# Two transformer blocks on one NeuronCore: in the mixers, the low part of a weight tile from a second, adding transfer in place of a subtraction

## The chip, the cores and the metric

The kernel runs on one core of a Trainium2 chip, as one program. The metric is the time of one execution on the device in microseconds; the lower the better. The median of three runs counts.

## What is computed

The reference runs two blocks one after the other on 512 tokens of width 1024, all in float32.

```python
def first_block(x, ...):                       # two layers
    for l in range(2):
        x = layer_norm(ALPHA * x + 0.5 * swiglu_ffn(x, ffn1_w_gu[l], ffn1_w_down[l]), ...)
        x = layer_norm(ALPHA * x + hybrid_mixer(x, w_in[l], w_out[l], ...), ...)
        x = layer_norm(ALPHA * x + 0.5 * swiglu_ffn(x, ffn2_w_gu[l], ffn2_w_down[l]), ...)
    return x

def second_block(x, meta_tokens, ...):         # one layer; 16 meta tokens go ahead of the 512
    h = concatenate([meta, x])
    h = h + 0.5 * swiglu(rmsnorm(h), w_gate, w_up, w_down)
    u = rmsnorm(h) @ w_in                      # differential attention and latent top-k attention
    ...
    h = h + concatenate([o_a, o_b]) @ w_out
    h = h + 0.5 * swiglu(rmsnorm(h), w_gate2, w_up2, w_down2)
    return h[16:]
```

`hybrid_mixer` projects with `w_in`, runs sliding-window attention (with sinks) and multi-scale retention side by side, and projects with `w_out`. So there are nine stages: FFN, mixer, FFN twice in the first block, and FFN, mixer, FFN in the second.

## The kernel before

**Precision.** TensorE multiplies in the type fp32r. Every operand is held as a high part (its copy in fp32r) and a low part (the value less that copy), and each product is three matmuls: high by high, high by low, low by high (`mm3`).

**Weights.** All weights lie in DRAM as one stream of 489 raw tiles of 128x1024 float32, 512 KB each, in the order of use. The class `Weights` (lines 56 to 276) brings them in. SyncE loads a raw tile into one of four buffers `wraw` (`_dma`). `_begin` then plans the two steps that make a split tile: ScalarE copies the raw tile to fp32r (high part), and then VectorE or GpSimd subtracts the high part from the raw tile (low part), whichever would be done sooner by the plan's clocks (`advance`). A raw buffer is free for the next load when its last step has been issued (`frees`). A split tile goes into one of four slots `wsplit` of its own, or into a slot `lent` by buffers that the stage does not need at the moment. A slot is free again when the last matmul that reads it is done. Most tiles of the FFNs have other kinds (S0 to S3, `SA`: sums of tiles for a product with seven multiplications in place of eight); in the mixers all tiles have the plain kind "W".

**Order.** The Python program writes each engine's instructions in their final order, and a planner (`Plan`) keeps a clock for each engine with a cost for each operation. `t["P"]` is TensorE's clock, `V`, `S`, `G` those of VectorE, ScalarE and GpSimd, `D` that of the transfers, `L` that of the port VectorE and GpSimd are taken to share. Side work (softmax, normalisation, splits) runs as generators that get their turn when the clocks say they are due (`run_due`, `tick`, `until`). Where the plan sees TensorE idle, `idle` writes filler matmuls (`m<-minus`, `s<-minus`, 128x256, results unused) in number for 0.8 of the gap at 0.118 us each. So any change of a cost or of a step moves the instructions around it, on all engines.

**Names.** `mixer1` (line 1396, called twice) and `mixer2` (line 1811) are the mixers, `ffn` (line 1029) the FFN. `acc`, `s`, `m` are PSUM tiles, `Z` the residual stream, `x` its normalised split, `y` (in the second block `yA`, `yB`) the mixer's output before the last projection, `rsq` a reciprocal root by a power on GpSimd, `pt` probabilities, `tb` a table of biases, `turned` and `sums` tiles of the FFN's special product. Nearly all instructions carry line 429, that of the helper that records them (`Engine`); they are told apart by their tiles.

Of the kernel before, what the change touches and what calls it, by code (L numbers as in the profile page):

```python
# [13 lines left out]
AF = mybir.ActivationFunctionType  # L14
OP = mybir.AluOpType
# [29 lines left out]
NEG = -1.0e30  # L45
GROUPS = ("T", "V", "more", "K1", "ya", "ic")
TAKEN = -3.0e38


class Step:  # L50
    def __init__(self, part, heavy, run, after, ready, frees):
        self.part, self.heavy, self.run, self.after, self.ready, self.frees = part, heavy, run, after, ready, frees
        self.issued, self.end = False, 0.0


class Weights:
# [7 lines left out]
    def __init__(self, nc, pool, kinds, src, plan, scalar, lo_engines):  # L64
        self.nc, self.pool, self.src = nc, pool, src
        self.plan, self.scalar, self.lo_engines = plan, scalar, lo_engines
        self.parts, r = [], 0
        for k in kinds:
            if k == "S0":
                pair, r = (r, r + 1), r + 2  # L70
            if k == "W":
                self.parts.append((k, (r,)))
                r += 1
            else:
                self.parts.append((k, pair))
        self.n_raw = r
        self.raw, self.arrives, self.spent, self.user = {}, {}, set(), {}
        for i, (k, rs) in enumerate(self.parts):
            for x in rs:
                self.user[x] = i  # L80
        self.ready, self.pending, self.chain = {}, [], {}
        self.n_dma = self.n_prep = self.n_get = 0
        self.free = deque(("own", f"w{i}") for i in range(4))
        self.lent, self.used = set(), {}
        self.fence = self.scr = None
        self.scr_last = []

    def lend(self, group, *tiles):

        self.lent.add(group)  # L90
        for t in tiles:
            if isinstance(t, tuple):
                self.free.append((group, t))
            else:
                for i in range(t.shape[1]):
                    self.free.append((group, (t[:, i, 0], t[:, i, 1])))
# [67 lines left out]
    def _begin(self, i, kind, rs, slot):  # L164
        if slot is not None:
            self.free = deque(x for x in self.free if x is not slot)
            self.used[slot[0]] = self.used.get(slot[0], 0) + 1
            if slot[0] == "own":
                t = self.pool.tile([128, 2, 1024], F32R, name="wsplit", tag=slot[1])
                hi, lo = t[:, 0], t[:, 1]  # L170
            else:
                hi, lo = slot[1]
            self.ready[i] = (slot, hi, lo)
        else:
            hi = lo = None
        at = max(self.arrives[r] for r in rs)
        raw = [self.raw.get(r) for r in rs]
        ch = self.chain

        def split(src, n, after=(), frees=(), ready=0.0):  # L180
            h = self._add(i, False, lambda: self.scalar.activation(hi[:, :n], src, AF.Copy), after, ready)
            return self._add(i, True, lambda e: e.tensor_sub(lo[:, :n], src, hi[:, :n]), [h], 0.0, frees)

        if kind == "W":
            split(raw[0], 1024, (), rs, at)
        elif kind == "S0":
            ch["lo"] = split(raw[0], 1024, (), (), at)
        elif kind == "SA":
            a, b = raw
            scr = self.scr  # L190
            one = self._add(i, True, lambda e: e.tensor_sub(scr[:, 512:], a[:, :512], b[:, :512]), self.scr_last, at)
            two = self._add(i, True, lambda e: e.tensor_add(b[:, :512], b[:, :512], b[:, 512:]), [one], at)
            six = self._add(i, True, lambda e: e.tensor_sub(scr[:, :512], b[:, :512], a[:, :512]), [two])
            ch.update(one=one, two=two, six=six)
        elif kind == "S1":
            ch["s1"] = split(self.scr, 1024, [ch["one"], ch["six"]])
        elif kind == "S2":
            split(raw[1], 1024, [ch["two"], ch["six"]], rs[1:])
        else:
            a, scr = raw[0], self.scr  # L200
            four = self._add(i, True, lambda e: e.tensor_sub(a[:, 512:], a[:, 512:], scr[:, :512]), [ch["six"], ch["lo"]])
            split(a[:, 512:], 512, [four], rs[:1])
            self.scr_last = [ch["s1"], four]
# [74 lines left out]
class Plan:  # L278
# [43 lines left out]
    def dma(self, ap, us):  # L322

        start = self.t["D"]
        name = ap.tensor.name
        if name in self.before:
            start = max(start, self._last(self.before.pop(name)) + 1.2)
        self.t["D"] = start + us
        c0 = ap.offset % ap.ap[0][0]
        c1 = c0 + 1 + sum((n - 1) * abs(d) for d, n in ap.ap[1:])  # L330
        self.used.setdefault(name, []).append((0, 128, c0, c1, start + us + 0.9, True, "D"))
        return start + us + 0.9 + self.LAG

    def op(self, e, us, writes, reads, shared=False):

        start = max(self.t[e], self.t["L"]) if shared else self.t[e]
        spans = []
        for ap, w in [(a, True) for a in writes] + [(a, False) for a in reads]:
            name, (ps, pn), free = ap.tensor.name, ap.ap[0], ap.ap[1:]
            if ps == 0:  # L340
                continue
            p0, c0 = divmod(ap.offset, ps)
            c1 = c0 + 1 + sum((n - 1) * abs(d) for d, n in free)
            if name in self.before:
                start = max(start, self._last(self.before.pop(name)) + self.LAG)
            for q0, q1, d0, d1, end, ew, ee in self.used.get(name, ()):
                if (w or ew) and q0 < p0 + pn and p0 < q1 and d0 < c1 and c0 < d1:
                    if ee != e:
                        start = max(start, end + self.LAG)
                    elif e != "P" and ew and not w:  # L350
                        start = max(start, end + 0.12)
            spans.append((name, p0, p0 + pn, c0, c1, w))
        end = self.t[e] = start + us
        if shared:
            self.t["L"] = end
        for name, q0, q1, d0, d1, w in spans:
            u = self.used.setdefault(name, [])
            if w:
                u[:] = [a for a in u if not (q0 <= a[0] and a[1] <= q1 and d0 <= a[2] and a[3] <= d1)]
            u.append((q0, q1, d0, d1, end, w, e))  # L360
        self.cur.end[e] = end
# [95 lines left out]
def build(ctx, tc, t, out, stop=None, dbg=None):  # L457
# [3 lines left out]
    V, S, G, PE = (Engine(plan, k, e) for k, e in zip("VSGP", (nc.vector, nc.scalar, nc.gpsimd, nc.tensor)))  # L461
# [22 lines left out]
    def have(room, shape=(128, 512), dtype=F32):  # L484

        while True:
            until(lambda: room.count() > 0)
            at, now = room.when(1), plan.t["P"]
            if at <= now + 0.2:
                break  # L490
            if not run_due():
                idle(min([at] + [due(j) for j in eligible() if due(j) > now]))
        return room.take(shape, dtype)
# [9 lines left out]
    W = Weights(nc, wpool, t["kinds"], t["w"], plan, S, (V, G))  # L503
# [525 lines left out]
    def ffn(halves, x, norm, newx, turned, source, sink=None, first=((0, 1, 2, 3),)):  # L1029
# [4 lines left out]
        if whole[0][1] > 512:  # L1034
            whole = halves
        n = halves[0][1] - halves[0][0]
        T = turned(n)
        W.take_back(*GROUPS)
        assert W.idle(*GROUPS)
        W.scr = T.scr  # L1040
        W.lend("more", *T.more)
        gates, H = {}, {}
# [63 lines left out]
        def seven(m, i, dst, beside):  # L1106
# [4 lines left out]
            def mult(p, w, k0, b, start):  # L1111
                for k in range(4):
                    mm3(p[:, :n], (w[0][:, k0 + k], w[1][:, k0 + k]), (b[0][:, k], b[1][:, k]),
                        start and k == 0, k == 3, **({} if start else dict(skip_group_check=True)))
                    tick()
# [19 lines left out]
            pb = have(accs)  # L1135
            mult(pb, w1, 0, T.t[2], True)
            j2 = then(over(q[:, 0], s[:, 0], pb, OP.add), j1)
# [9 lines left out]
            pc = have(accs)  # L1147
            mult(pc, w1, 4, T.t[3], True)
            W.done(w1)
            j4 = then(over(q[:, 1], q[:, 0], pc, OP.add), j2)  # L1150
            w2 = W.get("S2", (8, 128))
            pd = have(accs)
            mult(pd, w2, 0, T.t[1], True)
            j5 = then(over(u[:, 1], q[:, 1], pd, OP.add, True), j4)
# [239 lines left out]
        return d  # L1394

    def mixer1(l, x, norm):
        ready = set()
        W.take_back(*GROUPS)
        assert W.idle(*GROUPS)
# [409 lines left out]
    tokq = [(16 + 128 * i, 128) for i in range(4)]  # L1809

    def mixer2(x, norm):
        ready = set()
        W.take_back(*GROUPS)
        assert W.idle(*GROUPS)
# [716 lines left out]
```

## Time and profile before

| | |
|---|---|
| runs | 3102.7, 3108.1, 3113.8 us; median 3108.1 |
| profiled execution | 3105.4 us |
| its span, first to last instruction | 3103.5 us |
| TensorE's mean granted clock | 0.991 of full speed |
| busy share: TensorE, VectorE, ScalarE, GpSimd | 98%, 69%, 44%, 19% |
| mean share of the 16 transfer engines in use; rate | a quarter; 87 GB/s |

The stages lie, in us from the first instruction, at: FFN to 376, mixer to 613, FFN to 990, FFN to 1370, mixer to 1604, FFN to 2000, FFN (second block) to 2397, mixer to 2736, FFN to the end.

The busy time of TensorE includes the fillers, and the ends of its matmuls are modelled: a busy TensorE is not one that does useful work throughout. In a timeline a row gives the start, the time to the end of the group, engine and line, the operation, the written tile and those read, the shape and the count; in square brackets stand the idle time of that engine before it and what ended it.

### The profile page before, as it was taken

To read this page: it belongs to the slowest core of one execution; us is meant where nothing else is said; L and a number is where in the kernel's file an instruction comes from. 1 tells how busy PE (TensorE), PEld (TensorE's weight loads), DVE (VectorE), ACT (ScalarE), POOL (GpSimd) and SP (SyncE) were. 2 spreads that over 40 slices of the span, in tenths; PEclk is the share of its full clock that TensorE was granted. 3 is DMA by queue.
4 is the path that set the end of the run, shared out by engine and by line. 5 is a ranking of instruction groups with operands and counts; after the bars stand their busy time and mean duration, and the time that the engine had idled before them with its cause. 6 is when DMAs were issued, how large, how long until landed. Compare 5 with 4: busy or idle time off the path is not lost.

```text
span 3103.5 us, 51892 instructions
## 1 busy us (share of the span) xinstructions
PE 3043.5 (98%) x20797; PEld 2770.7 (89%) x20797; DVE 2149.0 (69%) x4209; ACT 1366.7 (44%) x2517; POOL 585.6 (19%) x411
## 2 busy tenths in 40 slices
PE   9999999999999999999999999999999999999999
PEld 8999987789999999997779999999999887889997
DVE  6767756587677766874567667486775886477774
ACT  4434464353344433447334434343343445544342
POOL 1121222212212122022321221111102111212110
PEclk9999999999999999999999999999999999999999
DMA  4333221113323233321211333223322110122332
GB/s 147 105 102 102 88 96 62 67 63 103 102 97 108 82 102 102 129 69 62 69 55 50 115 102 105 73 72 103 101 96 91 62 62 28 35 82 96 102 106 86
DMA packets 75553, 269.77 MB, mean 87 GB/s; under 512 B 8445, under 2 KB 10533, under 8 KB 75184
## 3 DMA queue, kind: packets, MB, share of 16 engines
q1 hardware_dynamic: 73712, 261.65, 25.3%
q0 software_dynamic: 1024, 3.75, 0.4%
q8 instruction: 164, 2.69, 0.4%
q10 hardware_dynamic: 576, 1.05, 0.1%
q14 instruction: 77, 0.63, 0.1%
HBM read 264.30 MB, written 3.68 MB: 86 GB/s over the span
## 4 chain that ended last, share of the span: by engine, by line
PE 73%; DVE 3%; issue 2%; ACT 2%; POOL 1%; DMA 0%; ACTq 0%; POOLq 0%; DVEq 0%
PE acc L429 65%; PE m L429 4%; PE s L429 4%; DVE wsplit L429 1%; DVE tmp L429 1%; DVE Z L429 1%; ACT wsplit L429 0%; POOL wsplit L429 0%; ACT tmp L429 0%; DVE x L429 0%; ACT Z L429 0%; POOL rsq L429 0%; DMA tb<-vr 0%; ACT x L429 0%; DVE y L429 0%
## 5 line engine op out<-in xcount | busy, mean ns | idle before, releaser
L429 PE MATMUL acc<-x,wsplit 128*128 128x256 f32 (+3 forms) x4248 | 598.0, 291 | 15.2 <-POOL x L429 5.3
L429 ACT ACTIVATE wsplit<-wraw 128x1024 fp32r<-128x1024 f32 (+1 forms) x455 | 423.7, 947 | 389.0 <-PE acc L429 353.0
L429 PEld LDWEIGHTS acc<-x,wsplit 128*128 128x128 f32 x4248 | 551.8, 190 | 35.1 <-POOL x L429 7.0
L429 PE MATMUL acc<-turned,wsplit 128*128 128x256 f32 (+1 forms) x4320 | 562.9, 283 | 8.2 <-DVE wsplit L429 6.8
L429 PEld LDWEIGHTS acc<-turned,wsplit 128*128 128x128 f32 x4320 | 538.5, 189 | 16.2 <-DVE wsplit L429 9.5
L429 DVE TENSOR_TENSOR wsplit<-wraw,wsplit 128x1024 fp32r<-128x1024 f32 (+1 forms) x381 | 408.0, 1076 | 129.1 <-ACT wsplit L429 126.9
L429 PE MATMUL acc<-H,wsplit 128*128 128x512 f32 (+2 forms) x2490 | 461.9, 338 | 0.7 <-DVE tmp L429 0.4
L429 PEld LDWEIGHTS acc<-H,wsplit 128*128 128x128 f32 x2490 | 379.5, 188 | 49.0 <-issue 1.9
L429 DVE TENSOR_TENSOR Z<-Z,acc 128x512 f32<-128x512 f32 (+2 forms) x295 | 165.7, 564 | 300.0 <-PE acc L429 299.1
L429 PE MATMUL acc<-wsplit,x 128*128 128x512 f32 (+3 forms) x1536 | 352.8, 380 | 0.0
L429 POOL TENSOR_TENSOR wsplit<-wraw,wsplit 128x1024 fp32r<-128x1024 f32 x74 | 180.5, 2439 | 912.8 <-ACT wsplit L429 847.4
L429 DVE TENSOR_TENSOR tmp<-tmp,acc 128x256 f32<-128x256 f32 (+1 forms) x570 | 238.7, 419 | 135.8 <-PE acc L429 129.5
L429 PEld LDWEIGHTS acc<-wsplit,x 128*128 128x128 f32 (+1 forms) x1536 | 260.0, 187 | 57.4 <-issue 1.4
L429 ACT ACTIVATE tmp<-acc 128x256 f32<-128x256 f32 (+2 forms) x278 | 108.6, 393 | 311.6 <-PE acc L429 301.4
L429 PE MATMUL acc<-H,turned 128*128 128x256 f32 (+2 forms) x1416 | 244.4, 327 | 0.0
L429 PEld LDWEIGHTS acc<-H,turned 128*128 128x128 f32 x1416 | 207.3, 189 | 20.8
L429 POOL TENSOR_TENSOR lent<-wraw,lent 128x1024 fp32r<-128x1024 f32 x45 | 110.9, 2465 | 573.7 <-ACT lent L429 550.7
L429 ACT ACTIVATE wsplit<-sums 128x1024 fp32r<-128x1024 f32 x90 | 95.3, 1059 | 234.3 <-DVE sums L429 233.8
L429 PE MATMUL acc<-x,lent 128*128 128x256 f32 (+1 forms) x1032 | 137.1, 282 | 0.0
L429 PEld LDWEIGHTS acc<-x,lent 128*128 128x128 f32 x1032 | 130.9, 188 | 2.4
L429 DVE TENSOR_TENSOR wsplit<-sums,wsplit 128x1024 fp32r<-128x1024 f32 x88 | 107.5, 1221 | 20.8 <-ACT wsplit L429 20.8
L429 DVE TENSOR_TENSOR sums<-wraw 128x512 f32<-128x512 f32 x171 | 117.3, 686 | 2.8 <-POOL wraw L429 1.6
(331 smaller groups left out, 4207.6 us busy)
## 6 DMA issues: line engine op xcount, KB each, us to landing
wraw<-in_w_dram SPq DMA_DIRECT2D x489, 512.0 KB, 3.3
decay<-in_decay_dram SPq DMA_DIRECT2D x4, 512.0 KB, 4.9
vr<-vr POOLq DMA_DIRECT2D x1, 1536.0 KB, 8.1
Z<-in_x_dram SPq DMA_DIRECT2D x4, 256.0 KB, 6.7
Z<-in_x_dram SPq DMA_DIRECT2D x2, 512.0 KB, 11.3
tb<-vr POOLq DMA_DIRECT2D x2, 512.0 KB, 4.1
out_dram<-Z SPq DMA_DIRECT2D x4, 256.0 KB, 2.0
out_dram<-Z ACTq DMA_DIRECT2D x4, 256.0 KB, 2.1
```

Of the source, the lines that this page charges most:

```text
L429: r = f(*args, **kw)
```

## The change

A flag `by_dma` of `Weights` is set at the start of each mixer and cleared at the start of each FFN. While it is set, a plain tile is split in another way. ScalarE copies the raw tile to fp32r, as before (high part). ScalarE copies it again with the factor -1 into the low part's place; with that the raw buffer is free. Then GpSimd issues a transfer that reads the same tile from DRAM once more and adds it to the low part's place, which then holds the tile less its high part. The subtraction on VectorE or GpSimd is gone. The planner gets a method `added` for the cost of the transfer: 1.0 us of GpSimd's clock, 1.46 of the transfers', and 0.9 to landing.

```diff
--- before.py
+++ after.py
@@ -84,6 +84,7 @@
         self.lent, self.used = set(), {}
         self.fence = self.scr = None
         self.scr_last = []
+        self.by_dma = False
 
     def lend(self, group, *tiles):
 
@@ -181,7 +182,16 @@
             h = self._add(i, False, lambda: self.scalar.activation(hi[:, :n], src, AF.Copy), after, ready)
             return self._add(i, True, lambda e: e.tensor_sub(lo[:, :n], src, hi[:, :n]), [h], 0.0, frees)
 
-        if kind == "W":
+        if kind == "W" and self.by_dma:
+            h = self._add(i, False, lambda: self.scalar.activation(hi, raw[0], AF.Copy), (), at)
+            g = self._add(i, False, lambda: self.scalar.activation(lo, raw[0], AF.Copy, scale=-1.0), [h], at, rs)
+
+            def add():
+                self.nc.gpsimd.dma_start(lo, self.src[rs[0]], accum_op=OP.add)
+                self.plan.added(lo, g.end)
+
+            self._add(i, False, add, [g])
+        elif kind == "W":
             split(raw[0], 1024, (), rs, at)
         elif kind == "S0":
             ch["lo"] = split(raw[0], 1024, (), (), at)
@@ -330,6 +340,15 @@
         c1 = c0 + 1 + sum((n - 1) * abs(d) for d, n in ap.ap[1:])
         self.used.setdefault(name, []).append((0, 128, c0, c1, start + us + 0.9, True, "D"))
         return start + us + 0.9 + self.LAG
+
+    def added(self, ap, after):
+
+        self.t["G"] = max(self.t["G"], after + self.LAG) + 1.0
+        self.t["D"] = max(self.t["D"], self.t["G"] - 1.46) + 1.46
+        end = max(self.t["D"], self.t["G"] + 1.46) + 0.9
+        c0 = ap.offset % ap.ap[0][0]
+        self.used.setdefault(ap.tensor.name, []).append((0, 128, c0, c0 + 1024, end, True, "D"))
+        self.cur.end["D"] = end
 
     def op(self, e, us, writes, reads, shared=False):
 
@@ -1034,6 +1053,7 @@
         if whole[0][1] > 512:
             whole = halves
         n = halves[0][1] - halves[0][0]
+        W.by_dma = False
         T = turned(n)
         W.take_back(*GROUPS)
         assert W.idle(*GROUPS)
@@ -1394,6 +1414,7 @@
         return d
 
     def mixer1(l, x, norm):
+        W.by_dma = True
         ready = set()
         W.take_back(*GROUPS)
         assert W.idle(*GROUPS)
@@ -1809,6 +1830,7 @@
     tokq = [(16 + 128 * i, 128) for i in range(4)]
 
     def mixer2(x, norm):
+        W.by_dma = True
         ready = set()
         W.take_back(*GROUPS)
         assert W.idle(*GROUPS)
```

Over the whole program 89 tiles change (79 in slots of their own, 10 in lent ones). VectorE loses 55 subtractions of a `wraw` from such tiles and GpSimd 34; ScalarE gains 89 copies, GpSimd 89 transfers of 512 KB. Of the fillers 463 are left of 491. SyncE's loads are the same. As every cost counts in the plan, much of the order in and just behind the mixers is written anew. The operations of the helper stand under line 448 in the changed kernel, the new transfer under line 190.

On ScalarE, behind the second layer's mixer, where the FFN begins (`lt` and `tmp` are the statistics of the normalisation, `Z` and `x` its result), the kernel before has:

```order
L429 ACTIVATE tmp<-Z 128x256 x8
L429 ACTIVATE wsplit<-wraw 128x1024
L429 ACTIVATE tmp<-Z 128x256
L429 ACTIVATE wsplit<-wraw 128x1024
L429 ACTIVATE turned<-wraw 128x1024
L429 ACTIVATE Z<-Z,lnp 128x256
L429 ACTIVATE x<-Z 128x256
```

and the changed kernel, from the copies ahead of the statistics on:

```order
L448 ACTIVATE tmp<-Z 128x256 x3
L448 ACTIVATE Z<-Z,lnp 128x256
L448 ACTIVATE x<-Z 128x256
L448 ACTIVATE Z<-Z,lnp 128x256
L448 ACTIVATE x<-Z 128x256
L448 ACTIVATE Z<-Z,lnp 128x256
L448 ACTIVATE x<-Z 128x256
L448 ACTIVATE Z<-Z,lnp 128x256
L448 ACTIVATE x<-Z 128x256
L448 ACTIVATE Z<-Z,lnp 128x256
L448 ACTIVATE x<-Z 128x256
L448 ACTIVATE wsplit<-wraw 128x1024 x2
```

Two weight copies that stood ahead of the first `Z` now stand behind the fifth `x`.

On GpSimd at the same seam, from the last `rsq` of the mixer on (`st` is a root of the normalisation), the kernel before has:

```order
L429 TENSOR_TENSOR rsq<-small,power 128x8
L429 TENSOR_TENSOR wsplit<-wraw,wsplit 128x1024
L429 TENSOR_TENSOR st<-st,power 128x2
L429 TENSOR_TENSOR wsplit<-wraw,wsplit 128x1024
L429 TENSOR_TENSOR turned<-wraw,turned 128x1024
L429 TENSOR_TENSOR x<-Z,x 128x256
```

and the changed kernel:

```order
L448 TENSOR_TENSOR rsq<-small,power 128x8
L190 DMA wsplit<-in_w_dram 128x1024 x4
L448 TENSOR_TENSOR lt<-lt,tmp 128x256
L448 TENSOR_TENSOR st<-st,power 128x2
L448 TENSOR_TENSOR x<-Z,x 128x256 x3
L448 TENSOR_TENSOR wsplit<-wraw,wsplit 128x1024
```

Four accumulating transfers stand where one subtraction stood, and three `x` come ahead of the first subtraction of the FFN.

On TensorE, in the last third of the second block's mixer (`cT`, `ql`, `cv` are the latents, `pza` and `pzb` the meta tokens' probabilities), the changed kernel has its longest row of fillers in that mixer's later part:

```order
L448 MATMUL acc<-wsplit,qb 128x256 x12
L448 MATMUL s<-minus 128x256 x6
L448 MATMUL m<-pt,cv 128x256 x6
L448 MATMUL m<-pza,cv 128x128
L448 MATMUL m<-pzb,cv 128x128
L448 MATMUL m<-pza,cv 128x128
L448 MATMUL m<-minus 128x256 x44
L448 MATMUL s<-identf,tmp 16x128
```

In the kernel before, the fillers of that part stand in seven smaller rows of 2 to 10. Over that whole mixer the fillers go from 151 to 167. In the first block's mixers, the 12 fillers ahead of each one's last transposes are gone, and nine matmuls stand between these and the transposes before.

## Rows read from the trace of the kernel before

**Rows 1.** the page: TensorE's busy time (part 1) and the chain by line (part 4).

```profile
PE 3043.5 (98%) x20797; PEld 2770.7 (89%) x20797; DVE 2149.0 (69%) x4209; ACT 1366.7 (44%) x2517; POOL 585.6 (19%) x411
...
PE acc L429 65%; PE m L429 4%; PE s L429 4%; DVE wsplit L429 1%; DVE tmp L429 1%; DVE Z L429 1%; ACT wsplit L429 0%; POOL wsplit L429 0%; ACT tmp L429 0%; DVE x L429 0%; ACT Z L429 0%; POOL rsq L429 0%; DMA tb<-vr 0%; ACT x L429 0%; DVE y L
```

**Rows 2.** stretches of the three mixers: bounds and length, each engine's busy time (instructions), granted clock, DMA share, GB/s.

```profile
376.00:613.00 237.00, 232.55 (x1196) 181.83 (x1195) 140.11 (x335) 120.67 (x259) 62.88 (x46) 0.99 0.21 69
1370.00:1604.00 234.00, 225.16 (x1149) 176.61 (x1148) 130.05 (x309) 110.78 (x242) 59.30 (x37) 0.97 0.19 63
2397.00:2736.00 339.00, 328.58 (x1995) 275.29 (x1994) 241.10 (x658) 170.77 (x429) 60.60 (x57) 0.98 0.15 50
```

**Rows 3.** weight tiles in the first mixer: count, shortest/median/longest ns, first and last start.

```profile
L429 ACT ACTIVATE wsplit<-wraw x26: 1040/1056/1065, 366.2 to 612.2; 128x1024 fp32r<-128x1024 f32 x26
...
L429 DVE TENSOR_TENSOR wsplit<-wraw,wsplit x16: 1211/1222/1227, 368.7 to 617.3; 128x1024 fp32r<-128x1024 f32 x16
...
L429 POOL TENSOR_TENSOR wsplit<-wraw,wsplit x9: 2363/2402/2413, 388.9 to 554.3; 128x1024 fp32r<-128x1024 f32 x9
```

**Rows 4.** timeline of the second mixer near 1515, GpSimd, VectorE and TensorE in turn.

```profile
1509.81 2.71 POOL L429 TENSOR_TENSOR rsq<-small,power 128x8 f32<-128x8 f32 x1 [2.48 <-DVE small L429]
...
1514.79 2.79 POOL L429 TENSOR_TENSOR wsplit<-wraw,wsplit 128x1024 fp32r<-128x1024 f32 x1
...
1512.56 2.83 DVE L429 TENSOR_TENSOR tmp<-tmp,rsq 128x512 f32<-128x512 f32 x1 [1.54 <-POOL rsq L429]
...
1515.42 2.71 DVE L429 TENSOR_TENSOR tmp<-tmp,sg 128x512 f32<-128x512 f32 x1
...
1518.27 1.09 PE L429 MATMUL m<-identf,tmp 128*128 128x128 f32 x4 [5.50 <-DVE tmp L429]
```

**Rows 5.** timeline at the end of the first mixer, VectorE and TensorE.

```profile
601.20 0.69 DVE L429 TENSOR_TENSOR tmp<-tmp,rsq 128x512 f32<-128x512 f32 x1 [1.75 <-POOL rsq L429]
...
600.94 1.50 PE L429 MATMUL m<-minus 128*128 128x256 f32 x12
```

**Rows 6.** first mixer: timeline of VectorE, TensorE's waits (total, times, longest), timeline.

```profile
533.35 2.88 DVE L429 TENSOR_TENSOR tmp<-tmp,rsq 128x512 f32<-128x512 f32 x1 [0.26 <-POOL rsq L429]
...
PE m L429 <- DVE tmp L429: 1.4, 2, 1.0
...
555.09 3.97 DVE L429 TENSOR_TENSOR y<-ya,y 128x512 fp32r<-128x512 f32 x4
...
557.30 2.13 PE L429 MATMUL acc<-y,lent 128*128 128x512 f32 x6 [1.70 <-DVE y L429]
```

**Rows 7.** timeline at the start of the FFN behind the first mixer, ScalarE and TensorE.

```profile
629.37 1.06 ACT L429 ACTIVATE wsplit<-wraw 128x1024 fp32r<-128x1024 f32 x1 [2.80 <-PE acc L429]
...
629.28 3.03 PE L429 MATMUL m<-minus 128*128 128x256 f32 x17
...
635.52 1.21 PE L429 MATMUL acc<-x,wsplit 128*128 128x256 f32 x8 [2.77 <-DVE x L429]
```

**Rows 8.** TensorE's waits from 2397 to 2745 (in total, times, longest).

```profile
PE s L429 <- DVE wsplit L429: 2.7, 2, 2.2
...
PE acc L429 <- DVE wsplit L429: 0.9, 1, 0.9
...
PE m L429 <- POOL wsplit L429: 0.7, 1, 0.7
...
PE acc L429 <- POOL wsplit L429: 0.6, 1, 0.6
```

**Rows 9.** the tile `tb`: its transfer's issue on GpSimd, shortest/median/longest ns.

```profile
L1793 POOL DMA_DIRECT2D tb<-vr x2: 802/808/814, 2377.5 to 2627.1; - x2
```

**Rows 10.** the page, part 6: transfers, KB each, median us from issue to landing.

```profile
wraw<-in_w_dram SPq DMA_DIRECT2D x489, 512.0 KB, 3.3
...
vr<-vr POOLq DMA_DIRECT2D x1, 1536.0 KB, 8.1
...
tb<-vr POOLq DMA_DIRECT2D x2, 512.0 KB, 4.1
```

## The prediction

> **What bounds the kernel now.** I began with the page. TensorE is busy for 98% of the span, and the chain of waits that ends last runs through its accumulating matmuls for 65% [rows 1]. So the kernel is a queue of matmuls, and an edit off TensorE pays only where TensorE stands still or does filler. Next I read the three mixers, the only places where the change acts, as stretches [rows 2]: of their 810 us TensorE works 786, so 24 us of waits are to be had there, plus whatever filler matmuls count as work. VectorE, ScalarE and GpSimd are busy for 63%, 50% and 23% of these stretches. Then I went through the stretches by time for TensorE's waits over 0.4 us and followed each to what came last. The weights are early nearly everywhere; the waits worth the name come from VectorE operations drawn out to four times their length beside a GpSimd subtraction, and from weight copies that stand ahead of the normalisation at a seam.
>
> **What the change removes.** Counted over the program's order, 89 of the mixers' weight tiles lose a subtraction (55 on VectorE, 34 on GpSimd). By [rows 3] a subtraction takes 1.22 us on VectorE and 2.40 on GpSimd: 67 and 82 us of engine time. Nearly all lies beside matmuls and is worth nothing by itself; its neighbours matter.
>
> A. Second layer, near 1518: TensorE waits 5.50 us for `tmp` [rows 4]. The two VectorE products before it took 2.83 and 2.71 us beside GpSimd subtractions (the one shown took 2.79), where the same product alone takes 0.69 [rows 5]; `rsq` ahead of them took 2.71. The product chain shortens by 2.14 + 2.02, and `rsq` by up to 1 us. I take -5.0 of the 5.5.
> B. First layer, same place: one product of 2.88 us [rows 6], and 1.03 us of TensorE wait behind it: -1.0.
> C. Both layers: four `y` operations on VectorE take 3.97 us with a GpSimd subtraction begun just ahead of them, and TensorE waits 1.70 [rows 6]. Alone, four take 4 x 0.69 = 2.8 us, 1.2 us less, and the first would end sooner too. The pattern stands twice: -1.5 each, -3.0.
> D. Both layers, end of the mixer: 12 fillers, 1.50 us [rows 5], put where the plan saw a gap before the last transposes. The new order has nine matmuls there and no filler: -1.5 each, -3.0.
> E. Both layers, start of the FFN behind: 17 fillers for 3.03 us and then a wait of 2.77 for `x` [rows 7]. ScalarE copies two weight tiles (1.06 us each [rows 3, 7]) ahead of the first `Z`, and a VectorE subtraction (1.22) stands ahead of its sums. In the new order five `Z`, `x` pairs come before these copies, and GpSimd makes three `x` before a subtraction. That is 2.1 + 1.2 = 3.3 us off the path; I take -3.0 for each of the two seams, -6.0. Bounds: 0, if the accumulates that GpSimd now issues just ahead hold its `x` back, and -11.6, if both gaps go whole.
> F. Start of the last FFN: two VectorE subtractions hold TensorE for 2.7 us [rows 8]; in the new order these tiles are ready sooner. -2.5.
>
> **What it adds.** ScalarE gets 89 more copies of 1.056 us [rows 3], 94 us on an engine that is half idle in these stretches. GpSimd issues 89 transfers; the nearest issue, of `tb`, occupies it for 0.81 us [rows 9], so 72 us for the 82 that it gives up. TensorE sees neither unless one is late.
>
> What it sees is the new path of a low part: 0.2 us after the slot is free, copy 1.06, copy 1.06, 0.1, then the accumulate's landing time L. No row shows an accumulate. From below, a plain load of the same 512 KB lands 3.3 us after its issue; from above, GpSimd's 1536 KB transfer takes 8.1, and its 512 KB one 4.1 [rows 10]. From the last two, a further 512 KB costs 2.0 us (4.0 us per 1024 KB). An accumulate of 512 KB also reads its target, and comes from GpSimd: it is nearest to the 4.1, plus something under the 2.0. I take L = 5.0, so the path is 7.4 us.
>
> Against this I laid, in the order of the changed kernel, how much matmul work lies between the last use of a tile's slot and its own first use. It is over 9.9 us for 65 of the 79 tiles with slots of their own; the ten in lent slots, which stand free for longer, I take to be no tighter. The tightest are four in the last third of the second block's mixer (3.0, 5.2, 6.6 and 6.9 us) and one of 7.4; then nine from 8.6 to 9.7. At L = 5.0 the first is 4.4 us late, its neighbour of 5.2 is covered by that same stall, and the two others are 0.8 and 0.5 late: +5.7.
>
> G. In that mixer three waits of 0.9, 0.7 and 0.6 us for weights go (-2.2) [rows 8]. Its fillers grow from 151 to 167: 16 x 0.125 (1.50 / 12, [rows 5]) = +2.0. With the late tiles: +5.5.
> H. The second copy shares ScalarE with the normalisations and exponentials, and an accumulate at the head of GpSimd's queue waits for it with `rsq`, `pt` and `x` behind. Nothing prices that; it lies between 0 and the 94 us of copies, and I put it near the bottom, as half of ScalarE's time is free: +5.
>
> The Trainium skill (DMA: Bandwidth & Descriptors, "Anatomy of one DMA — SWDGE (gpsimd) path") gives a transfer issued by GpSimd a fixed 2.0 us plus its bytes at 436 GB/s. By an estimate from that page, with the bytes counted twice, L would be 4.4 us, the late tiles +4.0 in place of +5.7, and the sum 1.7 us lower; its 3.2 us for a plain 512 KB is below the 4.1 of [rows 10], so the row was kept.
>
> Sum: -5.0 - 1.0 - 3.0 - 3.0 - 6.0 - 2.5 + 5.5 + 5.0 = -10.0. The profiled execution took 3105.4 us, so 3095.4. The median of the runs shown, 3108.1, stands 2.7 above it: forecast **3098 us**.
>
> The further 47 MB of reads are free: the transfer engines' share is 0.15 to 0.21 in the mixers [rows 2].
>
> **The rivals.** First, slower: **the accumulate lands late**. At L = 8.0 (the 8.1 of [rows 10]) the path is 10.4 us, and the tiles under that are late: 7.4 (covering its neighbour), 3.8, 3.5, 3.0, 1.8, 2.9 for the pair at 9.0, and 5.9 for the six from 9.2 to 9.7, 28.3 us in place of 5.7. Then the sum is -10.0 + 22.6 = +12.6, and the time 3121. It decides from L = 7.0 on, where the late tiles come to 16 us and the sum to zero. For it: the order of the changed kernel was laid out by a plan that reckons some 3.4 us from GpSimd's turn to landing, nearly what a plain load takes, so its fillers don't cover a longer one. Against it: the 4.1 us of a GpSimd transfer of this size.
> The Trainium skill (SBUF — State Buffer, "SBUF: two separate sides") warns that a transfer from GpSimd can stand until a VectorE operation gives back the port that both use. No row here shows one held; where it happens, L moves towards this rival.
>
> Second, **no change**: the waits are only renamed. Each of A to F ends a chain through `rsq`, ScalarE and the transposes, whose next member may be nearly as late; with half of A to F (-10) against the +10.5 of G and H the time is 3108. For it: 24 us of idle time in 810 is little, and the plan has put the rest of the order close. Against it: in A the next thing late was within 1 us, the drawn-out products being the whole wait.
>
> **How the numbers follow.** A measurement of this kernel can tell about 0.3% from no change, 9.3 us: faster is below 3098.8, slower above 3117.4. The forecast's case gets 0.52 (0.41 faster, 0.11 same, as it lies at the bound and H alone moves it by 5), the first rival 0.24 (0.19 slower, 0.05 same), the second 0.24 (0.02 faster, 0.19 same, 0.03 slower). Together: faster 0.43, same 0.35, slower 0.22. The range: with L = 3.3 the late tiles are 2.7 (-3), with H at 0 another -5, and with E whole -5.6, 3084 in all; upwards it takes in the first rival and 3 us more of H, 3124. The forecast's own case alone is 3084 to 3107.
>
> **What would show it.** Right: no VectorE product over 1 us in the first two mixers, TensorE's wait near the place of A under 1 us, accumulates landing in 4 to 6 us, one wait of some 4 us for an accumulate in the last third of the second block's mixer. Wrong: waits of TensorE for a transfer into `wsplit` at ten or more places (first rival); waits of the old sizes under other names, ScalarE or `rsq` above all (second); or a wait of GpSimd's `x` behind accumulates at the seams of E.

## The result: slower, and the profile after

The changed kernel takes 3156.4 us (median of four runs, 3151.9 to 3158.1) against 3105.4 for the kernel before (3101.9 to 3113.8): a ratio of 1.0149, 95% interval 1.0131 to 1.0167. The forecast was 3098, the range ended at 3124. The direction was that of the first rival, the size 35 us beyond it.

The page of the changed kernel has these lines for TensorE and the chain (parts 1 and 4) and for the transfer queues (part 3):

```profile
PE 3060.9 (97%) x20769; PEld 2783.7 (88%) x20769; DVE 2076.0 (66%) x4152; ACT 1449.1 (46%) x2606; POOL 572.7 (18%) x468
...
q1 hardware_dynamic: 73712, 261.65, 25.2%
q0 software_dynamic: 13840, 50.41, 8.6%
...
PE 74%; DMA 4%; DVE 2%; issue 2%; ACT 2%; POOL 0%; ACTq 0%; POOLq 0%; DVEq 0%
```

In [rows 1] transfers had 0% of the chain; now they have 4% of the span. Part 6 says which (KB each, median us from issue to landing):

```profile
wraw<-in_w_dram SPq DMA_DIRECT2D x489, 512.0 KB, 3.4
wsplit<-in_w_dram POOLq DMA_DIRECT2D x79, 512.0 KB, 8.2
lent<-in_w_dram POOLq DMA_DIRECT2D x10, 512.0 KB, 7.9
decay<-in_decay_dram SPq DMA_DIRECT2D x4, 512.0 KB, 8.5
```

The accumulate lands after 8.2 us; the sum had 5.0. And the four loads of `decay`, which the change does not touch, take 8.5 us (median of 5.8, 11.4, 5.7 and 11.2) where the page of before has them at 4.9:

```profile
decay<-in_decay_dram SPq DMA_DIRECT2D x4, 512.0 KB, 4.9
```

The three mixers as stretches, with the columns of [rows 2]:

```profile
376.00:621.00 245.00, 233.97 (x1190) 181.68 (x1189) 122.19 (x329) 146.58 (x290) 54.37 (x58) 0.99 0.51 121
1377.00:1615.00 238.00, 225.87 (x1142) 175.84 (x1141) 109.95 (x305) 138.24 (x273) 49.20 (x48) 0.96 0.50 118
2417.00:2790.00 373.00, 341.55 (x1993) 284.65 (x1993) 216.99 (x639) 200.50 (x461) 70.91 (x86) 0.94 0.40 93
```

The share of the transfer engines went from 0.15 to 0.21 to 0.40 to 0.51, far more than the bytes (63 and 69 GB/s became 118 and 121), and TensorE's granted clock in the second block's mixer fell from 0.98 to 0.94. TensorE's waits over the whole span (in total, times, longest) name two causes:

```profile
PE acc L448 <- DMA wsplit<-in_w_dram: 34.5, 18, 6.8
PE s L448 <- DVE tmp L448: 8.4, 2, 4.3
...
PE acc L448 <- DMA lent<-in_w_dram: 1.1, 1, 1.1
```

35.6 us are for accumulates. The 8.4 us look like VectorE's; the timeline of the first mixer shows what stands behind the first of the two (GpSimd, SyncE, VectorE and TensorE in turn):

```profile
551.51 0.86 POOL L190 DMA_DIRECT2D wsplit<-in_w_dram  x1 [13.37 <-ACT wsplit L448]
554.36 0.86 POOL L190 DMA_DIRECT2D wsplit<-in_w_dram  x1 [1.99 <-ACT wsplit L448]
557.14 0.85 POOL L190 DMA_DIRECT2D wsplit<-in_w_dram  x1 [1.93 <-ACT wsplit L448]
...
551.24 5.96 SPq L118 DMA_DIRECT2D wraw<-in_w_dram  x3
557.26 0.61 SPq L1413 DMA_DIRECT2D decay<-in_decay_dram  x1
...
568.70 0.42 DVE L448 TENSOR_TENSOR tmp<-s,decay 128x256 f32<-128x256 f32 x1 [5.25 <-DMA decay<-in_decay_dram]
...
569.67 1.51 PE L448 MATMUL s<-RT 64*128 64x256 f32 x6 [4.26 <-DVE tmp L448]
```

Three accumulates and three loads are under way when `decay` is issued at 557.26; it lands 11.4 us later, VectorE waits 5.25 for it and TensorE 4.26. The second layer has the same place, with 11.2 us.

To see where the 46 us between the two profiled executions lie, I cut both traces at the same matmuls (counted without fillers; us from one cut to the next). The last four columns are experiments described below.

| stretch | before | changed | no transfer | plain transfer | from buffer | VectorE only, first block |
|---|---|---|---|---|---|---|
| first mixer | 236.9 | 244.4 | 230.9 | 232.1 | 243.2 | 233.5 |
| second mixer | 234.0 | 237.6 | 219.0 | 219.3 | 229.5 | 222.7 |
| second block's mixer | 338.9 | 372.3 | 348.2 | 355.3 | 362.9 | 341.8 |
| the six FFNs | 2286.7 | 2288.9 | 2287.0 | 2284.8 | 2286.6 | 2292.3 |

Of the 46 us, 44 lie in the mixers, and 33 of these in the second block's.

### The profile page after: what moved, and what is told of

Read it like the earlier page. It is cut to its first block, busy times and chain, and to the rows that moved or that the text cites. A ratio compares the mean times of both kernels' runs of the same rounds, so it can differ in the third digit from the quotient of the medians.

```text
span 3149.9 us, 51989 instructions
## 1 busy us (share of the span) xinstructions
PE 3060.9 (97%) x20769; PEld 2783.7 (88%) x20769; DVE 2076.0 (66%) x4152; ACT 1449.1 (46%) x2606; POOL 572.7 (18%) x468
## 4 chain that ended last, share of the span: by engine, by line
PE 74%; DMA 4%; DVE 2%; issue 2%; ACT 2%; POOL 0%; ACTq 0%; POOLq 0%; DVEq 0%
PE acc L448 65%; PE m L448 5%; PE s L448 4%; DMA wsplit<-in_w_dram 3%; ACT wsplit L448 1%; DVE wsplit L448 1%; DMA decay<-in_decay_dram 1%; ACT tmp L448 1%; DVE Z L448 1%; DVE tmp L448 0%; ACT Z L448 0%; ACT x L448 0%; POOL x L448 0%; POOL tmp L448 0%; ACT ql L448 0%
## 5 line engine op out<-in xcount | busy, mean ns | idle before, releaser
L448 ACT ACTIVATE wsplit<-wraw 128x1024 fp32r<-128x1024 f32 (+1 forms) x533 | 501.1, 962 | 362.2 <-PE acc L448 325.5
L448 DVE TENSOR_TENSOR wsplit<-wraw,wsplit 128x1024 fp32r<-128x1024 f32 (+1 forms) x329 | 344.9, 1053 | 96.4 <-ACT wsplit L448 94.3
L448 ACT ACTIVATE tmp<-acc 128x256 f32<-128x256 f32 (+3 forms) x283 | 110.6, 393 | 327.0 <-PE acc L448 311.6
L448 POOL TENSOR_TENSOR wsplit<-wraw,wsplit 128x1024 fp32r<-128x1024 f32 x46 | 112.6, 2449 | 757.6 <-ACT wsplit L448 735.4
L448 POOL TENSOR_TENSOR lent<-wraw,lent 128x1024 fp32r<-128x1024 f32 x39 | 96.8, 2483 | 557.4 <-ACT lent L448 534.4
L190 POOL DMA_DIRECT2D wsplit<-in_w_dram x79 | 68.1, 862 | 348.2 <-ACT wsplit L448 259.6
## 6 DMA issues: line engine op xcount, KB each, us to landing
Z<-in_x_dram SPq DMA_DIRECT2D x2, 512.0 KB, 11.7
```

Source lines behind the costliest of these rows:

```text
L190: self.nc.gpsimd.dma_start(lo, self.src[rs[0]], accum_op=OP.add)
L448: r = f(*args, **kw)
```

## Experiments

**The ladder: no transfer, a plain transfer, the accumulate.** Theory: late accumulates, late `decay` and the lower clock cost the time. Rivals: the new order or the 89 copies on ScalarE cost it; or any second read does, added or not. These two kernels keep the changed kernel's order on every engine.

```diff
-                self.nc.gpsimd.dma_start(lo, self.src[rs[0]], accum_op=OP.add)
                 self.plan.added(lo, g.end)
```

> The changed kernel without its 89 transfers (the low part stays the negated high part, so the addition of the tile is left out), every engine's order otherwise the same. Theory, landing: the changed kernel lost its time to accumulates that land in 8.2 us in place of the 5.0 reckoned with, to the two waits behind late decay loads, and to the lower clock after those waits. Then this takes 3085 to 3105 us, TensorE has no wait for decay or a weight over 1 us beside those of before, and the stretches of A to F show their gain. Rival, order and ScalarE: the new order or the 89 further copies on ScalarE cost the time. Then it stays above 3135 us.

3096.6 us, ratio to before 0.9958 (0.9941 to 0.9975). So neither the order nor ScalarE's copies made the kernel slow. The products that A to C spoke of, in the second layer's mixer (count, busy us and mean ns, idle before):

```profile
L447 DVE TENSOR_TENSOR tmp<-tmp,rsq 128x512 f32<-128x512 f32 x4 | 2.8, 702 | 2.4 <-POOL rsq L447 2.4
L447 DVE TENSOR_TENSOR tmp<-tmp,sg 128x512 f32<-128x512 f32 x4 | 2.8, 692 | 0.1
L447 DVE TENSOR_TENSOR y<-ya,y 128x512 fp32r<-128x512 f32 x4 | 2.5, 686 | 0.1
```

None is drawn out any more; the ones of [rows 4, 6] took up to 2.9 us each. The second mixer is 15.0 us shorter than before, the first 6.0. The second block's mixer is 9.3 us longer even without transfers, with new waits in its new order:

```profile
PE m L447 <- DVE tmp L447: 3.8, 1, 3.8
PE s L447 <- DVE ql L447: 3.4, 2, 2.4
```

The next step writes the tile where the changed kernel adds it.

```diff
-                self.nc.gpsimd.dma_start(lo, self.src[rs[0]], accum_op=OP.add)
+                self.nc.gpsimd.dma_start(lo, self.src[rs[0]])
```

> The changed kernel with the same 89 transfers from GpSimd, each writing the tile in place of adding it (the addition is left out), order the same. Theory, the add: an accumulate holds the transfer engines about 2.9 us for 512 KB where a load holds them 1.5, and that is what makes it and its neighbours late. Then these land in 4.5 to 6 us, decay in 5 to 6.5, and the time is 3100 to 3125 us. Rival, the second read: any further 512 KB from GpSimd beside the load that the freed buffer lets go costs as much. Then they land in over 7 us and the time stays above 3140.

3100.4 us, ratio 0.9980 (0.9969 to 0.9992): a second read of the same bytes from the same engine in the same order costs 4 us by the medians. The addition costs some 53 more (ratio 1.0149 against 0.9980). Part 6 of its page, and TensorE's waits for these tiles:

```profile
wraw<-in_w_dram SPq DMA_DIRECT2D x489, 512.0 KB, 3.3
wsplit<-in_w_dram POOLq DMA_DIRECT2D x79, 512.0 KB, 4.6
lent<-in_w_dram POOLq DMA_DIRECT2D x10, 512.0 KB, 5.1
decay<-in_decay_dram SPq DMA_DIRECT2D x4, 512.0 KB, 6.2
...
PE acc L448 <- DMA wsplit<-in_w_dram: 10.7, 6, 4.0
```

and the first mixer's queues in the changed kernel (packets, MB, share of 16 engines over 245 us):

```profile
q0 software_dynamic: 3866, 14.85, 32.1%
q1 hardware_dynamic: 4032, 14.68, 18.4%
```

GpSimd's 27 accumulates hold all engines for 0.321 x 245 / 27 = 2.9 us each, SyncE's 29 loads of the same size for 0.184 x 245 / 29 = 1.55. The plain transfers hold them for

```profile
q0 software_dynamic: 3937, 15.13, 19.0%
```

0.190 x 234 / 27 = 1.6 us. (A few small transfers are counted in.) So the addition nearly doubles what a transfer takes of the engines. That is not an effect of the loads beside it, for in either kernel one transfer ran alone. Its packets in 7 us of each (changed kernel 510 to 517, plain transfers 506 to 513):

```profile
q0 software_dynamic: 144, 0.52, 43.5%
...
q0 software_dynamic: 144, 0.52, 23.0%
```

0.435 x 7 = 3.0 us against 0.230 x 7 = 1.6.

**From the buffer.** Sorting the 89 landings of the changed kernel by what ran between issue and landing: the one alone took 5.4 us; the 11 beside loads only, 7.8 (median); the 77 beside another accumulate too, 8.3, up to 11.7. The load beside it is its own: the negated copy frees the raw buffer, and SyncE's waiting load starts with the accumulate. This variant ties the load to the landing.

```diff
-            g = self._add(i, False, lambda: self.scalar.activation(lo, raw[0], AF.Copy, scale=-1.0), [h], at, rs)
+            g = self._add(i, False, lambda: self.scalar.activation(lo, raw[0], AF.Copy, scale=-1.0), [h], at)
...
-                self.nc.gpsimd.dma_start(lo, self.src[rs[0]], accum_op=OP.add)
+                self.nc.gpsimd.dma_start(lo, raw[0], accum_op=OP.add)
...
-            self._add(i, False, add, [g])
+            self._add(i, False, add, [g], 0.0, rs)
```

> The changed kernel with the raw buffer in SBUF as the source of the accumulate in place of a second read from DRAM; the buffer is then free only when the accumulate has landed. Theory, collision: nearly every accumulate of the changed kernel runs beside the load that its own negated copy has just let go (8.2 us; the one that ran alone took 5.4). Here that load starts behind it, so accumulates land in 5.4 to 6.5 us, decay in under 6, and the time is 3100 to 3130 us. Rival: the accumulate is as slow from SBUF, and four raw buffers held some 8 us longer make the loads and ScalarE's copies late; then 3140 us or more.

3124.1 us, ratio 1.0049 (1.0031 to 1.0066): two thirds of the loss are gone. Part 6, and TensorE's waits:

```profile
wsplit<-wraw POOLq DMA_DIRECT2D x79, 512.0 KB, 5.5
...
decay<-in_decay_dram SPq DMA_DIRECT2D x4, 512.0 KB, 6.5
...
PE acc L448 <- DMA wsplit<-wraw: 16.4, 7, 3.9
PE s L448 <- DVE tmp L448: 14.4, 2, 8.0
```

Landing and time came as the theory said, the waits for accumulates fell from 35.6 to 16.4; `decay` landed in 6.5, not under 6. The waits for it grew from 8.4 to 14.4 by another road: in SyncE's queue its load stands behind loads that now wait for a landing,

```profile
554.06 8.67 SPq L118 DMA_DIRECT2D wraw<-in_w_dram  x3
562.77 0.42 SPq L1413 DMA_DIRECT2D decay<-in_decay_dram  x1
```

and is issued 5.5 us later than in the changed kernel. The run changes the source and the load's start together. The 13 accumulates that ran alone took 4.5 us here (median). From DRAM the one of the changed kernel took 5.4, and three more in the two kernels with two raw buffers below took 5.0 to 5.3. So 0.5 to 0.9 of the 2.7 us may be the source's, and the rest fits the load's start.

**Every other tile.**

```diff
-        if kind == "W" and self.by_dma:
+        if kind == "W" and self.by_dma and i % 2:
```

> The changed kernel with the new split for every other tile only (by the tile's number in the stream), the rest split as before. Theory, queue: in a batch of four slots four accumulates and four loads hold the transfer engines 4 x (2.9 + 1.5) = 17.6 us against some 10.5 us of matmuls between the releases; with half of them it is 11.8, the queue all but goes, accumulates land in about 7 us, TensorE waits for them under 12 us in all, and the time is 3105 to 3122 us. Rival, each accumulate costs its half microsecond alike: half of the loss, 3128 to 3136 us.

3134.9 us, ratio 1.0078 (1.0047 to 1.0109), and the landing stayed at 8.0 us. The queue theory falls: the rival, a like cost for each accumulate, had 3128 to 3136. An accumulate needs no others to be slow: 23 of the 47 ran beside loads only and took 7.6 us (median), the other 24 took 8.2. The cost is not even, though. In the profile (3125.5 us, 9 under the median) the first two mixers are 8.3 and 11.0 us shorter than in the changed kernel and the second block's 2.6, and TensorE still waits 35.6 us for accumulates in all, as with 89 of them.

**Telling the plan.** If the plan had known the landing, would its order have covered it? Three prices, in `added`; the first also tells it of the engines' time:

```diff
-        self.t["D"] = max(self.t["D"], self.t["G"] - 1.46) + 1.46
-        end = max(self.t["D"], self.t["G"] + 1.46) + 0.9
+        self.t["D"] = max(self.t["D"], self.t["G"] + 1.5) + 2.9
+        end = self.t["D"] + 0.3
```

> The changed kernel with the plan told what the trace shows of an accumulate: 1.5 us from the end of the issue to its first packet, 2.9 us of the transfer clock, then landed. Theory, wrong price: the plan put matmuls ahead of weights it believed landed; told the truth it orders other work or fillers there, the waits of TensorE for transfers fall below 15 us in all (36 in the changed kernel), the clock stays up, and the time is 3105 to 3130 us. Rival, no slack: with six or seven slots of two raw buffers' worth the path is too long at any order; the waits come back under the fillers and the time stays above 3140.

```diff
-        end = max(self.t["D"], self.t["G"] + 1.46) + 0.9
+        end = max(self.t["D"], self.t["G"] + 1.46) + 5.7
```

> The changed kernel with the plan told of the later landing alone (5.7 us behind the issue in place of 0.9 and the transfer), and not of the transfer engines' time. Theory, the plan's transfer clock: the run with both prices lost 10 us more than the changed kernel because its plan put the loads later; without that the time is 3125 to 3150 us. Rival, no slack: four slots of their own set the distance from a slot's release to its next use (8.6 to 9.7 us at nine tiles in every one of these orders), and no price changes it; then 3150 to 3170.

```diff
-        end = max(self.t["D"], self.t["G"] + 1.46) + 0.9
+        end = self.t["G"] + 0.1
```

> The changed kernel with the plan told that an accumulate lands as soon as it is issued (no transfer time, no 0.9). With the plan told 5.7 us, the time rose by 30 us over the changed kernel, with both prices by 10. Theory, monotone: the later the plan believes a weight, the more of the matmuls that could cover the real landing it spends ahead of it; told nothing of the landing, the order comes out better, 3140 to 3152 us. Rival, no such trend: those two orders were worse by chance of the plan, and this one lies anywhere, within 10 us of the changed kernel or above it, 3150 to 3180.

3166.4 us (ratio 1.0188, 1.0167 to 1.0208), 3185.8 (1.0239, 1.0209 to 1.0268) and 3167.1 (1.0190, 1.0169 to 1.0211). None is better than the changed kernel, and there is no trend in the price. The waits for accumulates are 42.8, 51.7 and 39.9 us. None of the three prices makes room, as the rivals said; why the landing told truly gave the worst order of all, 3186, beyond even its rival, I did not find out.

**Five slots.** What sets the room is the number of slots. A fifth one needs 8 KB for each partition, which two raw buffers fewer give; so the control has two raw buffers and four slots.

```diff
-    RAW = 4
+    RAW = 2
```

> The changed kernel with two raw buffers in place of four: the control of the next run, which needs their room. The slots and the matmul work from a slot's release to its next use are as in the changed kernel (nine tiles at 8.6 to 9.7 us). Theory, slots: in the mixers TensorE waits for accumulates as in the changed kernel, 30 to 45 us in all; what two buffers cost beyond that falls into the FFNs, whose loads have less lead. Rival, buffers: it is the raw buffers' turn that makes weights late in the mixers too, and the waits there grow past 60 us.

```diff
-        self.free = deque(("own", f"w{i}") for i in range(4))
+        self.free = deque(("own", f"w{i}") for i in range(5))
```

> The changed kernel with two raw buffers and five slots of its own in place of four. The matmul work from release to next use is then over 10.3 us for all but five tiles. Theory, slots: with a path of some 10.4 us (0.2, two copies of 1.05, an accumulate of 8.2) TensorE's waits for accumulates in the mixers fall below 15 us, and the time is 20 us or more under that of the run with two raw buffers and four slots. Rival, transfer engines: accumulates and loads queue there whatever the slots, the landing grows with the lead, and the waits fall by less than 10 us.

3635.3 and 3592.3 us (ratios 1.1715, 1.1672 to 1.1757, and 1.1577, 1.1550 to 1.1604). Both are slow in the FFNs, where two raw buffers starve the subtractions, as expected of the control. TensorE's waits for accumulates, first with four slots:

```profile
PE acc L448 <- DMA wsplit<-in_w_dram: 33.6, 13, 8.8
PE acc L448 <- DMA lent<-in_w_dram: 3.9, 1, 3.9
```

and with five:

```profile
PE s L448 <- DMA wsplit<-in_w_dram: 8.9, 3, 5.3
PE acc L448 <- DMA wsplit<-in_w_dram: 8.5, 3, 5.8
```

37.5 us became 17.4, a little over the 15 expected, while the median landing stayed at 7.9 to 8.0. The three mixers together, cut as in the table, went from 865.5 to 825.5 us, which is the 43 us between the medians within 3. So the room from a slot's release to its next use, and not the transfer engines' queue, decides how much of the landing TensorE sees. Not all of the 40 us is that, as the plan wrote another order for five slots: 22 are TensorE's waits over 0.4 us in the mixers (58.1 to 36.1), and 61 fewer fillers in the second block's mixer make some 7.6 by an estimate at the prediction's 0.125 each. With two raw buffers the waits for accumulates stay at 37.5 and the three mixers grow from 854.3 to 865.5 us: the buffers' turn is not what makes most of these weights late.

**VectorE alone.** If the gain lies in GpSimd's subtractions going, no transfer is needed for it: the kernel before, with all subtractions of the mixers' tiles on VectorE.

```diff
-                    on_v = max(t["V"], t["L"]) + 1.1 < max(t["G"], t["L"]) + 2.3
+                    on_v = self.v_only or max(t["V"], t["L"]) + 1.1 < max(t["G"], t["L"]) + 2.3
...
     def mixer1(l, x, norm):
+        W.v_only = True
...
     def mixer2(x, norm):
+        W.v_only = True
```

with `v_only` cleared at the start of each FFN.

> The kernel before with all subtractions of the mixers' weight tiles on VectorE and none on GpSimd; no accumulate, no further copy. Theory, drawn-out products: the gain that the change could have had is the VectorE products lengthened beside GpSimd subtractions (A to C, some 9 us, and part of F). Then this is faster than before by 3 to 10 us: 3095 to 3103. Rival, VectorE is full: some 40 more subtractions of 1.22 us on VectorE, busy for 63% of the mixers, delay other work by as much, and the time is 3105 us or above.

3103.0 us, ratio 0.9985 (0.9976 to 0.9995). By the profiles the first two mixers gain 3.4 and 11.3 us and the second block's loses 4.1. So the next run sets it in `mixer1` alone:

> The kernel before with all subtractions of weight tiles on VectorE in the first block's two mixers alone. Theory: by the profiles, all on VectorE gained 3.4 and 11.3 us in these two and lost 4.1 in the second block's mixer and 2.7 ahead of it; so this takes 3093 to 3099 us and beats both kernels. Rival: these differences of single executions do not hold, and it is within 4 us of the run with VectorE alone throughout, 3099 to 3107.

3099.2 us, ratio 0.9960 (0.9946 to 0.9974). It is the fastest kernel of the study that computes the whole reference, though the time is at the edge between what the two expectations had. Its first two mixers, with the columns of [rows 2]:

```profile
376.00:609.00 233.00, 231.46 (x1193) 182.11 (x1192) 144.19 (x341) 119.14 (x257) 35.32 (x34) 0.99 0.21 69
1370.00:1592.00 222.00, 220.32 (x1155) 173.73 (x1154) 134.68 (x317) 111.59 (x243) 33.66 (x27) 0.99 0.21 67
```

VectorE is 4 to 5 us busier there than in [rows 2], and TensorE's idle time went from 4.5 and 8.8 us to 1.5 and 1.7. These two mixers gain 14.7 us by the table; the second block's mixer and the FFNs, where the flag is off, take 2.9 and 5.6 of it back.

## Why the prediction was wrong

**The step that failed is L.** The prediction took "L = 5.0 ... nearest to the 4.1, plus something under the 2.0". That bound of 2.0 came from a plain transfer with more bytes. The addition instead nearly doubles the time on the transfer engines (2.9 us for 1.6), and the landing is 5.4 us alone. What made it 8.2 is a step I saw in the diff and didn't follow: the negated copy frees the raw buffer, so a load starts beside the accumulate, nearly always. In the path of a tile this makes 0.2 + 2.1 + 0.1 + 8.2 = 10.6 us against room of 8.6 to 9.7 at nine tiles. The port of the prediction's first rival is not needed for it: the plain transfers, issued by GpSimd in the same order, land in 4.6.

The way from L to a wait was right at the tightest tile, at the end of the second block's mixer. There a landing of 7.5 us made TensorE wait 6.82, and a plain one of 4.6 made it wait 3.98, where the sum had 4.4 at L = 5.0:

```profile
2763.99 2.29 PE L448 MATMUL acc<-yA,wsplit 128*128 128x256 f32 x9 [6.82 <-DMA wsplit<-in_w_dram]
...
2713.64 0.62 PE L448 MATMUL acc<-yA,wsplit 128*128 128x256 f32 x3 [3.98 <-DMA wsplit<-in_w_dram]
```

And the plain transfers, which land about as L had it, give the forecast's time: ratio 0.9980, where 3098 to 3108.1 is 0.9967. That is in part luck, as their late tiles cost 10.7 us and not 5.7.

The estimate of 4.4 us from the Trainium skill (DMA: Bandwidth & Descriptors, "Anatomy of one DMA — SWDGE (gpsimd) path") was further off still: it reckons a transfer by itself, and no run here shows an accumulate that quick with DRAM as its source (the shortest took 5.0).

**The second is "the further 47 MB of reads are free".** The share of [rows 2] left room, but share is a mean: in the changed kernel it is 0.50 and 0.51, and in the burst shown above, from 551 to 569, it is 0.93. A load of SyncE's beside an accumulate lands in 5.8 us (median of 90; 3.3 for the 399 others), and `decay` in 11, which alone costs 8.4 us. The plain transfers moved the same bytes for 4 us in all, so it is not the bytes but the time that the additions hold the engines.

**The first rival had the mechanism and half the size.** It put 28.3 us of late tiles at L = 8.0 and 3121, and its sign was waits for a transfer into `wsplit` at ten or more places; there are 18. Against the run without transfers, in the cut traces, the changed kernel is 58.1 us longer: 38.6 in TensorE's waits over 0.4 us (43.7 for accumulates and behind `decay`, less 5.1 of others that are gone), and 19.5 in matmuls that follow each other more slowly, with the granted clock at 0.96 and 0.94 in the second and third mixer where the run without transfers has 1.00 and 0.97. The rival had neither `decay` nor this, and landings of up to 11.7 us in batches.

**The rest of the sum came out near, with luck.** Without its 5.7 us of late tiles it came to -15.7; the run without transfers, which keeps all else, is 12.4 us under before. But the terms miss both ways and cancel:
- A to D (-12.0): the two mixers are shorter by 21.0 us in that run; every drawn-out product is gone. Too small by 9, part of it the clock (0.97 to 1.00 in the second).
- E (-6.0): wrong. The gaps for `x` are gone, but the two FFNs behind are 1.3 us shorter and 2.0 longer: TensorE now waits at the seam for weights instead (1.94 us behind a GpSimd subtraction, at both).
- F (-2.5): the last FFN is 3.8 us shorter.
- G without late tiles (-0.2) and H (+5.0): the second block's mixer is 9.3 us longer, by its new order and the copies together; the runs don't divide it.

Of A to F the second rival, renamed waits, holds for E alone.

## What to carry to other kernels

Price a step by what its end lets go as well: a copy that frees a buffer starts a transfer at the very moment at which the next step wants the engines. Lay the whole path of a buffer, from release to ready, beside the work between release and next use; a plan can't cover what exceeds it, a slot more can. And when a change trades an operation for two others, try first whether moving the operation to another engine gives the same gain: here that gave 0.4% with no transfer at all, as much as the changed kernel without its transfers (ratios 0.9960 and 0.9958).

## What was not expected of the hardware

An adding transfer of 512 KB from GpSimd holds the transfer engines about 2.9 us, a writing one 1.6. It lands after 5.0 to 5.4 us from DRAM (four cases) and 4.5 from SBUF when nothing runs beside it, against 3.6 for a writing one (one case). Two loads of `decay` issued behind three of them took 11.4 and 11.2 us; behind plain transfers they took 6.8 and 6.7, and in the kernel before 5.7 and 5.1.
